# A two-layer trunk on one core: the memory's parts made in the FFN ahead of each mixer, another block order in first chunks, priorities on VectorE, narrower masks

## The chip, the cores and the metric

The kernel runs on one core of a Trainium2 chip, in one launch. The metric is the device time of that launch in microseconds (us); before the change it is 1129.36 us, the median of 3 runs (1125.65 to 1131.69). Engines are named as in the profile: PE is TensorE (matrix products), DVE is VectorE, ACT is ScalarE, POOL is GpSimd, and SP is SyncE, which issues the DMA transfers. DMA data go from HBM to SBUF; products land in PSUM, of which the kernel uses 8 banks.

## The reference

All values are float32: `x` is 1 x 256 x 1024, the memory `mem` 1 x 256 x 1024. Two layers run one after the other; layer 0 has a mixer of two attentions side by side, layer 1 multi-head latent attention. Cut to what matters here:

```
for layer in (0, 1):
    x = x + 0.5 * swiglu(rms_norm(x, ffn_norm[layer, 0]), ...)       # D_FF 2816
    h = rms_norm(x, mix_norm[layer])
    x = x + (diff_stickbreak_mixer(h, ...) if layer == 0 else mla_mixer(h, ...))
    x = x + memory_cross_attention(rms_norm(x, xm_norm[layer]), rms_norm(mem, xm_mem_norm[layer]), ...)
    x = x + 0.5 * swiglu(rms_norm(x, ffn_norm[layer, 1]), ...)

def rms_norm(x, gain):   return x * rsqrt(mean(x * x, -1) + 1e-6) * gain
def swiglu(h, wg, wu, wd):   return (silu(h @ wg) * (h @ wu)) @ wd
def memory_cross_attention(h, m, w_q, w_kv, ...):    # 4 heads of 128
    q = rms_norm(heads(h @ w_q));  k, v = split(m @ w_kv);  k = rms_norm(heads(k))
    return (softmax(q k^T / sqrt(128)) v) @ w_o
```

The mean of squares of the memory is the same in both layers; only the gain differs. In the chunk-causal softmax a query of chunk c (64 positions) sees the keys of chunks up to c, in query blocks of 128.

## The kernel before

**Exact products in three passes.** Every float32 factor is split into a high part in the chip's fp32r type and a low part, the rest. A block product is then three single-pass matmuls into one PSUM tile (`mm3`, L275 to L279): high x high (L276), high x low (L277) and low x high (L278). Weights come from HBM in pieces of 1 MB (`wr`); ACT casts the high part (`wh`, L240) and DVE subtracts (`wl`, L242; in the mixers POOL takes a quarter). There are two raw buffers (`RAW`), three pairs of high and low parts (`HL`), and a weight is asked for two ahead of its use (`LOOK`). The release of a weight's buffers by PE is thus what lets ACT begin with a later weight.

**Phases.** FFN, mixer, cross-attention, FFN in each layer. Read from the trace: the first FFN to 204 us, the first mixer to 339.6, its cross-attention to 381, the second FFN to 577, the FFN of layer 1 to about 765, the second mixer (MLA) to 893, its cross-attention to 934.6, the last FFN to the end. x is held as 8 blocks of 128 features x 256 positions. An FFN makes gate and up products in 11 pairs of chunks of 256 columns, then 8 down products; a chunk product is 2 column halves (j) x 8 row blocks (k) of `mm3`, in the order j = 0: k = 0 to 7, then j = 1 (`fm`, L584; in mixers the generator `fm_g`, L596).

**From one phase to the next.** The last products of a phase add to x block by block in `finish_dt` (L491): DVE adds the PSUM tile to x (L494), which also frees the PSUM bank; `split` makes the high part on ACT (`xh`, L471) and the low part on DVE (`xl`, L472) with the next norm's gain; ACT squares (L505) and POOL sums the squares over the blocks (L513). The norm's scale is applied behind the next product. `norm` (L522) sums the squares over partitions with PE (`colsum`, L465), DVE adds epsilon (L525), POOL takes the power (L457). `spread` (L531) brings the scale to all partitions: two diagonal matrices on DVE (L534), one product with ones on PE (L537), a copy by ACT (L539).

**Memory.** `mem_gain` (L755) loads the transposed memory in four transfers of 256 KB (L761) and splits its 8 blocks (L471, L472) into buffers named slotr. It is called in the mixers: in the first one behind the second product, in MLA at the first memory product. In the first mixer, ACT also squares the memory (L770), POOL adds the squares (L773, L776), and PE sums them over partitions in a task of its own (`colsum`, L465), of which the scale follows. The keys and values of the memory are then made in the mixers.

**Who sets the order.** In mixers and cross-attentions the PE order is written by a planner (`run`, L430): tasks are generators with a priority (lower first) and conditions; each event has an estimated time (tables `EST_*`), and of the tasks that may start by then, the one with the lowest priority goes next. On the other engines a scheduler orders the instructions, mostly as the code emits them; `tc.high_priority()` moves those inside it forward, and `keep_in_program_order` pins one to its place. Each engine works its queue strictly in that order, and so does SP with the transfers it issues.

**Masks.** `mask` (L308) writes -1e30 into the scores' tile by a product of two rows, ahead of the scores: for query block 0 (t = 0) 512 columns (L310), for block 1 256 columns (L312).

**Table.** ACT loads the table of the exponential and logarithm in the first mixer ahead of its use (L950). In MLA it is loaded at the first exponential (L729).

## Time and profile before

| | |
|---|---|
| median of 3 runs (lowest to highest) | 1129.36 us (1125.65 to 1131.69) |
| profiled execution, its own time | 1128.84 us |
| its span, from first to last instruction | 1127.1 us |
| granted PE clock, mean over the span | 0.997 of full |
| busy: PE, DVE, ACT, POOL | 1102.8, 776.8, 653.3, 199.8 us |
| share of the span: PE, DVE, ACT, POOL | 98%, 69%, 58%, 18% |
| moved by DMA | 192.44 MB, mean 171 GB/s |

How to read it: one execution was recorded instruction by instruction; the times in the rows below count from the span's start. A busy PE counts overlapping matmuls once. A wait is put down to the instruction that released it last. In timelines a row may join several instructions (xN) and gives start, duration, and in brackets the engine's idle time ahead and who ended it.

### The profile page before, as it was taken

The page shows a single profiled execution, that of the slowest core. Times are in us where ns is not written, and L with a number is a line of the kernel's source. Part 1 is how long each engine was busy: PE and PEld are TensorE (multiplying, and loading weights), DVE is VectorE, ACT ScalarE, POOL GpSimd, SP SyncE. Part 2 cuts the span into 40 slices and gives each one's busy share as a digit, 9 for nine tenths or more (in the row PEclk, how much of TensorE's full clock was granted, in tenths as well). Part 3 has the DMA queues.
Part 4 walks back from the last instruction along what each step waited for, and adds up shares of the span by engine and source line. Part 5 has one row for each costly group of instructions (what it writes and reads, how often), then busy time and mean ns, then how long its engine had stood idle before and what let it go on. Part 6 is the DMA issues. An engine that isn't in the chain of part 4 may idle for free.

```text
span 1127.1 us, 23381 instructions
## 1 busy us (share of the span) xinstructions
PE 1102.8 (98%) x9044; PEld 1083.6 (96%) x9044; DVE 776.8 (69%) x1865; ACT 653.3 (58%) x1771; POOL 199.8 (18%) x217
## 2 busy tenths in 40 slices
PE   8999999999999999999999999999989999999998
PEld 8999999898999999999999999999878999999998
DVE  6867665768876776675666766655788768676653
ACT  6655545676765665554555555546866566555542
POOL 2000001556343200000100000014861421000000
PEclk9999999999999999999999999999999999999999
DMA  8654545544454345555545454555341534555561
GB/s 299 220 195 176 188 170 184 192 140 151 121 166 163 129 171 187 187 179 183 195 172 207 169 198 167 191 178 192 108 145 45 164 135 148 190 187 188 178 210 62
DMA packets 50224, 192.44 MB, mean 171 GB/s; under 512 B 5696, under 2 KB 7360, under 8 KB 35008
## 3 DMA queue, kind: packets, MB, share of 16 engines
q1 hardware_dynamic: 50112, 190.94, 49.7%
q8 instruction: 71, 1.16, 0.4%
q14 instruction: 41, 0.34, 0.1%
HBM read 189.87 MB, written 1.05 MB: 169 GB/s over the span
## 4 chain that ended last, share of the span: by engine, by line
PE 83%; DVE 9%; ACT 2%; issue 2%; POOL 2%; DMA 1%; SPq 0%; DVEq 0%; POOLq 0%; ACTq 0%
PE mm L276 26%; PE mm L277 26%; PE mm L278 26%; DVE wl L242 4%; DVE xl L472 1%; DMA wr<-wflat 1%; PE t L742 1%; POOL sm L457 1%; ACT wh L240 1%; DVE x L494 1%; PE t L465 1%; PE s L880 0%; PE o L1452 0%; PE s L1419 0%; ACT xh L471 0%
## 5 line engine op out<-in xcount | busy, mean ns | idle before, releaser
L240 ACT CAST wh<-wr 128x256 fp32r<-128x256 f32 (+1 forms) x1216 | 440.0, 433 | 337.8 <-PE mm L277 307.9
L242 DVE TENSOR_TENSOR wl<-wr,wh 128x256 fp32r<-128x256 f32 (+1 forms) x1171 | 482.6, 470 | 117.9 <-ACT wh L240 112.8
L276 PE MATMUL mm<-xh,wh 128*128 128x256 f32 x1584 | 447.7, 283 | 4.3 <-DVE slotf L682 1.8
L277 PE MATMUL mm<-xl,wh 128*128 128x256 f32 x1584 | 445.5, 281 | 3.6 <-DVE xl L472 3.6
L278 PE MATMUL mm<-xh,wl 128*128 128x256 f32 x1584 | 445.6, 281 | 0.1
L276 PEld LDWEIGHTS mm<-xh,wh 128*128 128x128 f32 x1584 | 299.3, 189 | 5.5 <-issue 3.2
L277 PEld LDWEIGHTS mm<-xl,wh 128*128 128x128 f32 x1584 | 299.4, 189 | 4.6 <-DVE xl L472 4.4
L278 PEld LDWEIGHTS mm<-xh,wl 128*128 128x128 f32 x1584 | 299.2, 189 | 0.6 <-DVE wl L263 0.3
L276 PE MATMUL mm<-slotr,wh 128*128 128x256 f32 x896 | 252.4, 282 | 0.0
L277 PE MATMUL mm<-slotr,wh 128*128 128x256 f32 x896 | 251.4, 281 | 0.0
L278 PE MATMUL mm<-slotr,wl 128*128 128x256 f32 x896 | 251.4, 281 | 0.0
L276 PEld LDWEIGHTS mm<-slotr,wh 128*128 128x128 f32 x896 | 168.9, 188 | 0.4 <-issue 0.3
L277 PEld LDWEIGHTS mm<-slotr,wh 128*128 128x128 f32 x896 | 168.9, 189 | 0.1
L278 PEld LDWEIGHTS mm<-slotr,wl 128*128 128x128 f32 x896 | 168.9, 188 | 0.0
L513 POOL TENSOR_TENSOR acc<-acc,sq 128x256 f32<-128x256 f32 x49 | 40.5, 827 | 538.2 <-ACT sq L505 531.8
L242 POOL TENSOR_TENSOR wl<-wr,wh 128x512 fp32r<-128x512 f32 x45 | 67.7, 1505 | 108.8 <-ACT wh L240 108.7
L690 DVE TENSOR_TENSOR slotf<-mm,rb 128x512 f32<-128x512 f32 x44 | 30.4, 690 | 81.9 <-PE mm L278 81.9
L682 DVE TENSOR_TENSOR slotf<-mm,rb 128x512 f32<-128x512 f32 x44 | 30.4, 690 | 38.0 <-PE mm L278 38.0
L276 PE MATMUL mm<-wh,slotr 128*128 128x256 f32 (+2 forms) x176 | 55.5, 315 | 0.0
L471 ACT ACTIVATE xh<-x,gains 128x256 fp32r<-128x256 f32 x64 | 32.0, 506 | 39.2 <-DVE x L494 35.4
L278 PE MATMUL mm<-wh,slotr 128*128 128x256 f32 (+2 forms) x176 | 53.3, 303 | 0.0
L277 PE MATMUL mm<-wl,slotr 128*128 128x256 f32 (+2 forms) x176 | 53.1, 302 | 0.0
(192 smaller groups left out, 1095.7 us busy)
## 6 DMA issues: line engine op xcount, KB each, us to landing
wr<-wflat SPq DMA_DIRECT2D x118, 1024.0 KB, 4.8
wr<-wflat SPq DMA_DIRECT2D x180, 256.0 KB, 3.9
wr<-wflat SPq DMA_DIRECT2D x16, 768.0 KB, 4.3
slotf<-memT SPq DMA_DIRECT2D x8, 256.0 KB, 5.5
x<-xT SPq DMA_DIRECT2D x4, 256.0 KB, 4.6
wr<-wflat SPq DMA_DIRECT2D x2, 512.0 KB, 7.7
slotf<-xtok SPq DMA_DIRECT2D x4, 256.0 KB, 7.7
out<-x SPq DMA_DIRECT2D x8, 128.0 KB, 3.8
```

The source lines that it names most:

```text
L240: A.copy(hi[:, a:b], raw[:, a:b])
L242: e.tensor_tensor(out=lo[:, a:b], in0=raw[:, a:b], in1=hi[:, a:b].bitcast(F32), op=ALU.subtract)
L276: PE.matmul(out, a[0], b[0], start=first, stop=False, **kw)
L277: PE.matmul(out, a[0], b[1], start=False, stop=False, **kw)
L278: PE.matmul(out, a[1], b[0], start=False, stop=last, **kw)
L457: G.tensor_tensor(out=y, in0=v, in1=mhalf[:, 0:n], op=ALU.pow)
L465: PE.matmul(ps[:, 2 * c:2 * c + 2], b, ones[:, 0:2], start=k == 0, stop=k == len(blocks) - 1)
L471: return (A.activation(hi, src, AF.Identity, scale=g), V.scalar_tensor_tensor(out=lo, in0=src, scalar=g, in1=hi.bitcast(F32), op0=ALU.mult ...
L472: V.scalar_tensor_tensor(out=lo, in0=src, scalar=g, in1=hi.bitcast(F32), op0=ALU.mult, op1=ALU.subtract))
L513: G.tensor_tensor(out=st.acc, in0=st.acc, in1=sq, op=ALU.add)
L682: V.tensor_tensor(out=t.rearrange("p (a b) -> p a b", b=S), in0=pg.rearrange("p (a b) -> p a b", b=S), in1=rbb, op=ALU.mult)
L690: V.tensor_tensor(out=u.rearrange("p (a b) -> p a b", b=S), in0=pu.rearrange("p (a b) -> p a b", b=S), in1=rbb, op=ALU.mult)
```

## The change

Five things change.

1. **Memory.** The call of `mem_gain` moves into `ffn`: in the first FFN of each layer, after the pairs f = 2, 4, 6 and 8 (`MEM_AT`), a quarter of the memory is loaded and split, into eight tiles of its own that stay (`mem0h` to `mem3l`). For layer 0 a second copy of the memory, with positions on partitions (`memtok`), is loaded too (four transfers of 256 KB), and ACT squares it with the sum over the features taken along; two DVE instructions and a power on POOL give the scale. The adds on POOL, the column sums on PE and their task are gone. The arenas of the mixers have 11 slotr buffers instead of 19.
2. **Block order.** The first chunk of each phase (`gate` of f = 0 in an FFN but the very first, `qb` 0, `ckv`, `xq` 0) takes the blocks in the order EARLY: k = 0 to 4 of j = 0, k = 0 to 4 of j = 1, then k = 5 of both j, 6 of both, 7 of both.
3. **Priorities.** The update of x, its splits, the norm's DVE instructions and the scalings in `spread` are emitted with `tc.high_priority()`.
4. **Masks.** Only the columns that the mask changes are written: the last 64 of each 128 (t = 0) or of each 256 (t = 1): 256 and 128 columns.
5. **Table.** MLA asks for the exponential's table behind its first product; the scheduler puts it ahead of the last high part of x in the FFN before; the request in the first mixer stays.

The diff, cut to its core:

```diff
-SLOTS_MLA = (29, 19)
+SLOTS_MLA = (29, 11)          # SLOTS_MIX likewise
+MEM_AT = (2, 4, 6, 8)
...
     def mask(sp, t, b, n):
-        if t == 0:
-            PE.matmul(sp, mq[b:b + n], mk[b:b + n], start=True, stop=False, skip_group_check=True)
-        else:
-            PE.matmul(sp.rearrange("p (a b) -> p a b", b=S)[:, :, P:S], mq[b:b + n], mk[b:b + n, 0:S],
-                      start=True, stop=False, skip_group_check=True)
+        w = P if t == 0 else S
+        PE.matmul(sp.rearrange("p (a b) -> p a b", b=w)[:, :, w - 64:w], mq[b:b + n], mk[b:b + n, 0:512 * 64 // w],
+                  start=True, stop=False, skip_group_check=True)
...
     def finish_dt(dt, gc, ps=None, factor=1.0):
         xd = x[:, dt, :]
         if ps is not None:
-            V.scalar_tensor_tensor(out=xd, in0=ps, scalar=factor, in1=xd, op0=ALU.mult, op1=ALU.add)
+            with tc.high_priority():
+                V.scalar_tensor_tensor(out=xd, in0=ps, scalar=factor, in1=xd, op0=ALU.mult, op1=ALU.add)
...
-        made = split(h, l, xd, gcol(gc + dt))
         st.nxt[dt] = (h, l)
         if ps is None:
-            return made
+            return split(h, l, xd, gcol(gc + dt))
+        with tc.high_priority():
+            split(h, l, xd, gcol(gc + dt))
...          # norm (tensor_scalar, rsqrt) and spread (both scalings) likewise under high_priority
+    EARLY = [(j, k) for j in range(2) for k in range(KT - 3)] + [(j, k) for k in range(KT - 3, KT) for j in range(2)]
+    PLAIN = [(j, k) for j in range(2) for k in range(KT)]
-    def fm(w, xg, between=None):
+    def fm(w, xg, between=None, order=PLAIN):
         ps = ps_("mm")
-        for j in range(2):
-            if j and between:
+        for j, k in order:
+            if (j, k) == (1, 0) and between:
                 between()
-            for k in range(KT):
-                mm3(ps[:, j * S:(j + 1) * S], (w[0][:, j * KT + k, :], w[1][:, j * KT + k, :]),
-                    xg[k], k == 0, k == KT - 1)
+            mm3(ps[:, j * S:(j + 1) * S], (w[0][:, j * KT + k, :], w[1][:, j * KT + k, :]),
+                xg[k], j == k == 0 if order is EARLY else k == 0, k == KT - 1, skip_group_check=order is EARLY)
...          # fm_g likewise; callers pass EARLY for gate of f = 0, ("qb", 0), ("xq", 0), ckv
+    def mem_gain(l, q):
+        raw = al()
+        nc.sync.dma_start(raw.rearrange("p (a b) -> p a b", b=S), memT_d[:, 2 * q:2 * q + 2, :])
+        h, lo = mem_hl[2 * q:2 * q + 2]
...
+        for j in range(2):
+            sl_ = slice(j * S, (j + 1) * S)
+            split(h[:, sl_], lo[:, sl_], raw[:, sl_], gcol(G_MEM + l * KT + 2 * q + j))
+            memstate["x"].append((h[:, sl_], lo[:, sl_]))
+        rel(raw)
+        if l:
+            return
+        mt = al()
+        nc.sync.dma_start(mt, memtok_d[:, q // 2, (q % 2) * 512:(q % 2 + 1) * 512])
+        A.activation(mt, mt, AF.Square, accum_out=msum[:, q:q + 1])
...          # q == 3: tensor_reduce, tensor_scalar, rsqrt -> memstate["rs"]
     def ffn(l, j, gc, need_rb, mem=None):
...
+            if mem is not None and f in MEM_AT:
+                mem_gain(mem, MEM_AT.index(f))
...
-            ps = yield from fm_g("ckv", xg)
+            ps = yield from fm_g("ckv", xg, EARLY)
+            tc.keep_in_program_order(A.preload_act_table_set("natural_log_exp_and_others"))
```

Line numbers of the changed kernel are a few off: its `wl` is L243, its `mm3` L277 to L279, its update of x L495, the norm's DVE instruction L528, the scalings L538. Three places show what moves.

The first is VectorE at the start of the first mixer, around the spread. In the rows before, slotr from slotf are the memory's low parts, `sl_2669` is the norm's variance, L534 are the two scalings, and `wl` are weight splits:

```order
L472 SCALAR_TENSOR_TENSOR slotr_2705<-slotf_2679,gains,slotr_2704 128x256 x2
L525 TENSOR_SCALAR sl_2669<-t_2791 128x2
L472 SCALAR_TENSOR_TENSOR slotr_2707<-slotf_2682,gains,slotr_2706 128x256
L534 TENSOR_SCALAR slotf_2688<-cst,sl_2668 128x128
L242 TENSOR_TENSOR wl_2797<-wr_2796,wh_2798 128x512 x3
L534 TENSOR_SCALAR slotf_2688<-cst,sl_2668 128x128
L472 SCALAR_TENSOR_TENSOR slotr_2707<-slotf_2682,gains,slotr_2706 128x256
L472 SCALAR_TENSOR_TENSOR slotr_2709<-slotf_2684,gains,slotr_2708 128x256 x2
L472 SCALAR_TENSOR_TENSOR slotr_2711<-slotf_2686,gains,slotr_2710 128x256 x2
```

The same place in the changed kernel:

```order
L364 TENSOR_TENSOR nlam<-lam 128x1
L365 TENSOR_SCALAR nlam<-nlam 128x1
L528 TENSOR_SCALAR sl_2711<-t_2825 128x2
L538 TENSOR_SCALAR slotf_2721<-cst,sl_2710 128x128 x2
L243 TENSOR_TENSOR wl_2831<-wr_2830,wh_2832 128x512 x3
```

The memory's low parts are gone from here, and the two scalings stand together, ahead of the three weight splits that stood between them.

The second is TensorE in the first chunk of the second FFN, the gate product. Before, the block `xh_4997`, the last of x (k = 7), comes as the eighth `mm3`, and j = 1 starts behind it:

```order
L278 MATMUL mm_5063<-xh_4976,wl_4798 128x256
L276 MATMUL mm_5063<-xh_4997,wh_4799 128x256
L277 MATMUL mm_5063<-xl_4998,wh_4799 128x256
L278 MATMUL mm_5063<-xh_4997,wl_4798 128x256
L276 MATMUL mm_5063<-xh_4845,wh_4799 128x256
```

In the changed kernel, behind the fifth `mm3` (`xh_4930`, k = 4) the order goes back to the first block (`xh_4841`); the last block's `xh_4993` comes in the 15th and 16th `mm3`, at the chunk's end:

```order
L277 MATMUL mm_5059<-xh_4930,wh_4795 128x256
L278 MATMUL mm_5059<-xl_4931,wh_4795 128x256
L279 MATMUL mm_5059<-xh_4930,wl_4794 128x256
L277 MATMUL mm_5059<-xh_4841,wh_4795 128x256
L278 MATMUL mm_5059<-xl_4842,wh_4795 128x256
L279 MATMUL mm_5059<-xh_4841,wl_4794 128x256
```

The third is VectorE at the same phase's start: the updates of x (x from mm), the low parts of x (`xl`) and the splits of the next two weights. Before:

```order
L494 SCALAR_TENSOR_TENSOR x<-mm_4920,x 128x256
L242 TENSOR_TENSOR wl_4901<-wr_4900,wh_4902 128x256 x5
L472 SCALAR_TENSOR_TENSOR xl_4935<-x,gains,xh_4934 128x256
L494 SCALAR_TENSOR_TENSOR x<-mm_4941,x 128x256
L494 SCALAR_TENSOR_TENSOR x<-mm_4962,x 128x256
L472 SCALAR_TENSOR_TENSOR xl_4956<-x,gains,xh_4955 128x256
L494 SCALAR_TENSOR_TENSOR x<-mm_4983,x 128x256
L472 SCALAR_TENSOR_TENSOR xl_4977<-x,gains,xh_4976 128x256
L242 TENSOR_TENSOR wl_5044<-wr_5043,wh_5045 128x256
L472 SCALAR_TENSOR_TENSOR xl_4998<-x,gains,xh_4997 128x256
```

After:

```order
L495 SCALAR_TENSOR_TENSOR x<-mm_4916,x 128x256
L243 TENSOR_TENSOR wl_4897<-wr_4896,wh_4898 128x256 x3
L495 SCALAR_TENSOR_TENSOR x<-mm_4937,x 128x256
L472 SCALAR_TENSOR_TENSOR xl_4931<-x,gains,xh_4930 128x256
L243 TENSOR_TENSOR wl_4897<-wr_4896,wh_4898 128x256
L472 SCALAR_TENSOR_TENSOR xl_4952<-x,gains,xh_4951 128x256
L495 SCALAR_TENSOR_TENSOR x<-mm_4958,x 128x256
L243 TENSOR_TENSOR wl_4897<-wr_4896,wh_4898 128x256
L472 SCALAR_TENSOR_TENSOR xl_4973<-x,gains,xh_4972 128x256
L495 SCALAR_TENSOR_TENSOR x<-mm_4979,x 128x256
L243 TENSOR_TENSOR wl_5040<-wr_5039,wh_5041 128x256 x3
L472 SCALAR_TENSOR_TENSOR xl_4994<-x,gains,xh_4993 128x256
```

The update of the second of these four blocks (`x` from mm_4941 before, mm_4937 after) stands behind three weight splits of this stretch instead of five and behind no low part; the last low part stands behind three pieces of the weight after next instead of one.

## Rows read from the trace of the kernel before

**Rows 1.** The page, part 1: busy time, share of the span, instructions of each engine.

```profile
PE 1102.8 (98%) x9044; PEld 1083.6 (96%) x9044; DVE 776.8 (69%) x1865; ACT 653.3 (58%) x1771; POOL 199.8 (18%) x217
```

**Rows 2.** The waits of TensorE: who, for whom, us in total, times, longest.

```profile
PE mm L277 <- DVE xl L472: 3.6, 4, 1.0
PE s L1419 <- DVE slotf L1406: 2.7, 1, 2.7
...
PE t L742 <- DVE slotf L734: 2.0, 1, 2.0
...
PE mm L276 <- DVE x L494: 0.8, 2, 0.7
...
PE s L1034 <- ACT slotf L1059: 0.6, 1, 0.6
```

**Rows 3.** Timeline of TensorE, start of the first mixer: start, us, instruction, [idle before].

```profile
213.03 0.28 PE L278 MATMUL mm<-xh,wl 128*128 128x256 f32 x1
215.62 0.67 PE L537 MATMUL t<-slotf,ones 128*128 128x256 f32 x2 [2.31 <-issue]
```

**Rows 4.** Timeline of VectorE at the same place.

```profile
211.69 0.29 DVE L534 TENSOR_SCALAR slotf<-cst,sl 128x128 f32<-128x128 f32 x1 [0.61 <-POOL sl L457]
211.89 2.96 DVE L242 TENSOR_TENSOR wl<-wr,wh 128x512 fp32r<-128x512 f32 x3
214.78 0.74 DVE L534 TENSOR_SCALAR slotf<-cst,sl 128x128 f32<-128x128 f32 x1
```

**Rows 5.** Timeline of TensorE, the memory's column sums in the first mixer.

```profile
223.17 0.50 PE L465 MATMUL t<-ones,slotf 128*128 128x2 f32 x4
224.15 0.49 PE L1034 MATMUL s<-slotf,slotf 64*128 64x256 f32 x2 [0.48 <-DVE slotf L957]
```

**Rows 6.** Timeline of TensorE, start of the first cross-attention.

```profile
342.09 0.28 PE L276 MATMUL mm<-xh,wh 128*128 128x256 f32 x1
343.34 0.39 PE L277 MATMUL mm<-xl,wh 128*128 128x256 f32 x1 [0.97 <-DVE xl L472]
```

**Rows 7.** Stretches: busy us (instructions) of each engine, granted clock, DMA share, GB/s.

```profile
45.00:65.00 20.00, 20.00 (x171) 20.00 (x170) 13.81 (x35) 9.88 (x30) 0.00 (x0) 1.00 0.55 190
...
28.00:34.00 6.00, 5.09 (x30) 5.12 (x31) 6.00 (x16) 5.20 (x15) 0.30 (x2) 0.72 0.61 197
820.50:828.50 8.00, 5.35 (x26) 4.40 (x26) 6.13 (x11) 3.86 (x7) 6.87 (x7) 0.79 0.59 189
```

**Rows 8.** Groups by line, 204 to 222 us: busy us, mean ns | idle before.

```profile
L472 DVE SCALAR_TENSOR_TENSOR slotr<-slotf,gains,slotr 128x256 fp32r<-128x256 f32 x8 | 5.5, 742 | 3.1 <-ACT slotr L471 3.1
L776 POOL TENSOR_TENSOR slotf<-slotf,slotf 128x256 f32<-128x256 f32 x6 | 5.4, 895 | 0.4
...
L471 ACT ACTIVATE slotr<-slotf,gains 128x256 fp32r<-128x256 f32 x8 | 3.7, 498 | 2.7 <-DMA slotf<-memT 2.7
```

**Rows 9.** Timeline of TensorE, masks of 512 and of 256 columns in MLA.

```profile
824.78 0.38 PE L312 MATMUL s<-mk,mq 128*128 128x256 f32 x1
824.98 0.61 PE L1419 MATMUL s<-slotf,slotf 96*128 96x256 f32 x1
...
834.19 0.48 PE L310 MATMUL s<-mk,mq 128*128 128x512 f32 x1
834.51 0.50 PE L1419 MATMUL s<-slotf,slotf 96*128 96x128 f32 x3
```

**Rows 10.** Timeline of ScalarE, the first exponentials of MLA.

```profile
827.95 1.28 ACT L729 ACT_TABLE_LOAD   x1 [2.85 <-DVE sm L723]
```

**Rows 11.** Groups by line, 45 to 105 us in the first FFN.

```profile
L240 ACT CAST wh<-wr 128x256 fp32r<-128x256 f32 x84 | 27.9, 402 | 27.6 <-PE mm L277 25.9 <-issue 1.6
```

**Rows 12.** Groups by line, 0 to 60 us: squares of x at the start.

```profile
L1494 ACT ACTIVATE slotf<-slotf 128x512 f32<-128x512 f32 x4 | 2.5, 619 | 0.0
```

**Rows 13.** Groups by line, 762 to 776 us: the memory's low parts in MLA.

```profile
L472 DVE SCALAR_TENSOR_TENSOR slotr<-slotf,gains,slotr 128x256 fp32r<-128x256 f32 x8 | 3.4, 476 | 3.1 <-ACT slotr L471 3.1
```

**Rows 14.** The page, part 6: transfers, KB each, us from issue to landing.

```profile
slotf<-memT SPq DMA_DIRECT2D x8, 256.0 KB, 5.5
```

More of the change, by code (lines that the diff above doesn't have):

```diff
@@ L68 @@
 HL = 3
[L69 removed]
+SLOTS_MIX = (29, 11)
+MEM_AT = (2, 4, 6, 8)
 def _cols(w, c0, c1):
@@ L326, in rows @@
             return rows_a[:, c0:c0 + w] if c0 < 384 else rows_b[:, c0 - 384:c0 - 384 + w]
-        for dst, c0, w in ((mq, C_MQ, P), (mk, C_MK, 512), (ntri, C_TRI, P)):
+        for dst, c0, w in ((mq, C_MQ, P), (mk, C_MK, S), (ntri, C_TRI, P)):
             tmp = al()
@@ L524, in norm @@
             v = st.var
-            V.tensor_scalar(out=v, in0=cs, scalar1=1.0 / D, scalar2=EPS, op0=ALU.mult, op1=ALU.add)
-            rsqrt(v, 2, st.rs)
+            with tc.high_priority():
+                V.tensor_scalar(out=v, in0=cs, scalar1=1.0 / D, scalar2=EPS, op0=ALU.mult, op1=ALU.add)
+                rsqrt(v, 2, st.rs)
             return ps
@@ L532, in spread @@
         dg = al()
-        for t in range(2):
-            V.tensor_scalar(out=dg[:, t * P:(t + 1) * P], in0=ident, scalar1=st.rs[:, t:t + 1],
-                            scalar2=None, op0=ALU.mult)
+        with tc.high_priority():
+            for t in range(2):
+                V.tensor_scalar(out=dg[:, t * P:(t + 1) * P], in0=ident, scalar1=st.rs[:, t:t + 1],
+                                scalar2=None, op0=ALU.mult)
         ps = get("t")
@@ L598, in fm_g @@
         ps = take("mm")
-        for j in range(2):
-            for k in range(KT):
-                mm3(ps[:, j * S:(j + 1) * S], (w[0][:, j * KT + k, :], w[1][:, j * KT + k, :]),
-                    xg[k], k == 0, k == KT - 1)
-                if k % 4 == 3 and (j, k) != (1, KT - 1):
-                    yield {}
+        for i, (j, k) in enumerate(order):
+            mm3(ps[:, j * S:(j + 1) * S], (w[0][:, j * KT + k, :], w[1][:, j * KT + k, :]),
+                xg[k], j == k == 0 if order is EARLY else k == 0, k == KT - 1, skip_group_check=order is EARLY)
+            if i % 4 == 3 and i < 2 * KT - 1:
+                yield {}
         done(key)
@@ L669, in ffn @@
         for f in range(FT // 2):
-            pg = fm_first(xg) if ("gate", l, j, f) == FIRST else ahead or fm(weight(("gate", l, j, f), P), xg)
+            pg = (fm_first(xg) if ("gate", l, j, f) == FIRST else
+                  ahead or fm(weight(("gate", l, j, f), P), xg, order=PLAIN if f else EARLY))
             ahead = None
@@ new lines, in trunk_kernel @@
+    mem_hl = [cpool.tile([P, 512], F32R, name=f"mem{q}{h}") for q in range(4) for h in "hl"]
+    memstate["rs"] = cpool.tile([P, 2], F32, name="rmem")
+    msum = cpool.tile([P, 4], F32, name="msum")
+    def mem_gain(l, q):
+        raw = al()
+        nc.sync.dma_start(raw.rearrange("p (a b) -> p a b", b=S), memT_d[:, 2 * q:2 * q + 2, :])
+        h, lo = mem_hl[2 * q:2 * q + 2]
+        if q == 0:
+            memstate["x"] = []
+        for j in range(2):
[8 more added lines that the diff above has]
+        A.activation(mt, mt, AF.Square, accum_out=msum[:, q:q + 1])
+        rel(mt)
+        if q == 3:
+            v = sm()[:, 0:2]
+            V.tensor_reduce(out=v, in_=msum.rearrange("p (a b) -> p a b", b=2), axis=AX.X, op=ALU.add)
+            V.tensor_scalar(out=v, in0=v, scalar1=1.0 / D, scalar2=EPS, op0=ALU.mult, op1=ALU.add)
+            rsqrt(v, 2, memstate["rs"])
@@ L854, in products @@
             for c in range(2):
-                ps = yield from fm_g((f"xq{l}", c), xg)
+                ps = yield from fm_g((f"xq{l}", c), xg, PLAIN if c else EARLY)
                 q = al()
@@ L947, in products @@
                 for c in range(2):
-                    ps = yield from fm_g((key, c), xg)
+                    ps = yield from fm_g((key, c), xg, EARLY if (key, c) == ("qb", 0) else PLAIN)
                     if (key, c) == ("qb", 0):
@@ L971, in products @@
                     c = int(key[1])
-                    yield from (mem_k(0, c, [ev["rm"]]) if key[0] == "k" else
-                                mem_v(0, c, memstate["v"], Event(), [ev["rm"]]))
+                    yield from (mem_k(0, c, []) if key[0] == "k" else
+                                mem_v(0, c, memstate["v"], Event(), []))
                     continue
@@ L1359, in mem_product @@
         def mem_product(c):
-            if c == 0:
-                mem_gain(1, ev)
             yield from mem_k(1, c, [])
-            if c == 1 and not MEM_KEEP:
-                rel(*memstate.pop("tiles"))
         def mem_values(c):
@@ L1527, in _constants @@
             c[:, cs + t * d:cs + (t + 1) * d] = np.concatenate([-sin[r], sin[r]], 1)
-    kk = np.arange(512)
     for row in (0, 64):
         c[row, C_MQ:C_MQ + 64] = -1e30
-        c[row, C_MK:C_MK + 512] = kk % 128 >= 64
+        c[row, C_MK:C_MK + S] = 1.0
     return c
```

70 lines of the change are left out of this document (11 added, 59 removed).

## The prediction

> **What bounds the kernel now.** I read the page's busy times first: TensorE is busy for 98% of the span [rows 1], so time is gained only where TensorE waits, or from what it executes. The second view is the list of TensorE's waits [rows 2]. The reader is to see that no wait there is longer than 2.7 us, and that most are for results of VectorE. Third come timelines of places where the change acts: the start of the first mixer [rows 3, 4], the memory's column sums there [rows 5], and the start of a cross-attention [rows 6]. Inside an FFN TensorE never waits: from 45 to 65 us it is busy for all 20.00 us with 171 matmuls [rows 7], so one 128x256 matmul comes every 20.00/171 = 0.117 us. A wait costs the distance between the two starts around it, less this pace.
>
> The sum is made against the profiled execution, 1128.84 us (the span of 1127.1 and 1.74 around it), which is 0.5 below the median of 1129.36.
>
> **Start of the first mixer.** The spread matmul of L537 starts 215.62 − 213.03 = 2.59 us after its predecessor [rows 3], 2.47 more than the pace. It needs both diagonal scalings of L534. The first runs at 211.69, the second at 214.78, behind 2.96 us of weight splits [rows 4]; ahead of them VectorE and GpSimd work off the memory's splits and squares [rows 8]. The change puts both scalings right behind the norm. Started together at 211.69 at the latest, they end by 211.69 + 2 × 0.29 = 212.3, before TensorE comes to the spread at 213.03 + 0.12. Term: −2.47. What is late next is the weight split behind them, by 0.29 us, for a weight whose product is still to come.
>
> The column sums of the memory's squares (L465) and the wait behind them leave TensorE: 224.15 − 223.17 = 0.98 us [rows 5]. The scores behind them waited 0.48 us for VectorE; four more blocks of three matmuls (12 × 0.117 = 1.4 us) now stand ahead of them and cover that. Term: −0.98.
>
> The planner puts the rest of this mixer in another order. The largest other wait there that the list names is 0.6 us (L1034 for L1059 [rows 2]), the best case if it goes. The worst that I can bound is one new wait as long as the longest on a VectorE result, 2.7 us [rows 2]. I take −0.4, near the best: VectorE and GpSimd have eight splits and seven additions less there, and no row shows the new wait.
>
> **Starts of four phases.** In the two cross-attentions and the two second FFNs, one matmul of the first chunk waits for the low part of the last block of x: 3.6 us over 4 waits [rows 2]. Between starts one of them costs 343.34 − 342.09 − 0.12 = 1.13 for a named wait of 0.97 [rows 6], so 0.16 comes on top of each: 3.6 + 4 × 0.16 = 4.24. Before, block 7 is due after 7 blocks of three matmuls; in the order of after it is due after 14, so 7 × 3 × 0.117 = 2.46 us later. The longest of the four waits is 1.0 [rows 2], and where the chunk itself starts earlier it is by 0.8 at most (next term): 0.6 us are in hand, even if no split comes earlier. The order of after also puts VectorE's updates and splits of x ahead of weight splits. Blocks 5 and 6 are due after 10 and 12 blocks instead of 5 and 6, 1.8 and 2.1 us later, and before neither was waited for. Term: −4.24.
>
> The first matmul of both second FFNs waits for an update of x that frees its PSUM bank: 0.8 named over 2 waits, the longest 0.7 [rows 2], with 0.16 each on top 1.12. The order of after puts that update behind six weight splits instead of eight and a split of x, over 1 us earlier. Term: −1.12. Late next are the weight splits that these pass, a few pieces, for a product that starts 48 × 0.117 = 5.6 us after the chunk.
>
> **Masks.** Of the 18 mask matmuls, 6 shrink from 512 columns to 256 and 12 from 256 to 128. A 512-column one is followed 0.32 us later, a 256-column one 0.20 us later [rows 9]: 0.12 less. One of the six stands ahead of the 2.7 us wait, which swallows it: 5 × 0.12 = 0.60. For 128 columns there is no row: each gives 0.06 (half of 0.12) if columns set the pace and 0 if what follows does, so the 12 give 0 to 0.72. I take half; together −0.96, bounds −0.6 to −1.32.
>
> **Table load in the second mixer.** ACT loads its table for 1.28 us once its wait for VectorE is over, and the first exponential stands behind it [rows 10]. The order of after has the load in the FFN before, ahead of the last split of x. TensorE's wait of 2.0 us for the normalised result (L734) [rows 2] hangs on these exponentials, but L734 also stands behind weight splits on VectorE. Bounds 0 and −1.28; I take −0.8, since the order of after also moves L734 ahead of a weight split. In the FFN the load delays ACT by 1.28 us, where in 60 us it idles 27.6 for TensorE [rows 11].
>
> **Work added to the FFNs.** For two layers × 8 blocks of the memory: 16 high parts on ACT at 0.50 us [rows 8] and 16 low parts on VectorE; four squares of 0.62 us [rows 12] with their sums read on ACT; 8 + 4 transfers of 256 KB. The low part took 0.74 us in the first mixer, beside GpSimd's additions [rows 8], and 0.48 us in the second, without them [rows 13]. In the FFN GpSimd does nothing [rows 7], so I take 0.48. The Trainium skill (SBUF — State Buffer, section Who interferes with whom) says that a VectorE instruction with two SBUF inputs contends with a GpSimd instruction that reads SBUF. Both rows agree, and by it the price in the FFN is 0.48; by the first mixer's row it would be 16 × 0.26 = 4.2 us more of VectorE's time, as hidden as the rest. One call costs ACT 1.0 to 1.8 us and VectorE 1.0 us. From 45 to 65 us ACT is busy for 9.88 of 20 us and VectorE for 13.81 [rows 7], and ACT's idle time ends with TensorE's release of a weight buffer, at least one product (5.6 us) ahead of that weight's use. Term: 0. From the second mixer the same splits vanish: also 0, since no wait of TensorE stands there, and the later 2.7 us wait (L1419 for L1406) hangs on a chain whose order is not changed.
>
> **Sum.** −2.47 − 0.98 − 0.4 − 4.24 − 1.12 − 0.96 − 0.8 = −10.97; 1128.84 − 10.97 = 1117.9, forecast 1118.
>
> **Rivals.**
> A, the waits come back in part. Only half of the 5.36 us at the four starts goes, because the wait moves to another block or to a weight split that was passed, and the first mixer's new order costs 2.7 where I have −0.4. Then 1117.9 + 2.68 + 3.1 = 1123.7; with one of the two, 1120.6 or 1121.0. For it: the planner's times for that order are estimates, and a low part there can take twice as long beside GpSimd. Against: the time in hand above.
> B, the other side: in-order blocking in the FFN. A memory transfer lands 5.5 us after its issue [rows 14], and ACT's high part waits for it with the weight's casts behind it, for which VectorE and then TensorE wait. ACT idles 27.6 us before 84 casts [rows 11], which are 10.5 weights, 2.6 us each. If nothing else hid it, each of the 8 calls would stop TensorE for 5.5 − 2.6 = 2.9 us: 1117.9 + 23.2 = 1141. It decides for slower from (11.0 + 5.6)/8 = 2.1 us per call. Against: the 5.6 us between a weight's casts and its use, and a share of 0.55 of the DMA engines at 190 GB/s [rows 7]; 3.1 MB more at 190/0.55 = 345 GB/s are 9.1 us of their time over two FFNs. The Trainium skill (Trainium Kernel Development and Optimization, section Key Constraints) says that transfers of all queues run on the same 16 engines and interleave, so by it a memory transfer also lengthens a weight's landing; no row of before shows the two together inside an FFN, and that is why B is not nearer 0.
> C, the clock: TensorE's granted clock averages 0.72 in 28 to 34 us and 0.79 in 820.5 to 828.5 [rows 7], which is about 3.4 us at the lower level (1.2 GHz) in each, after waits of TensorE. Where work fills them they cost half, 1.7 us. If they go, 1116.2 (one) or 1114.5 (both). Against: the waits ahead of both are not touched.
>
> **How the numbers follow.** Forecast 64% (its own range 1115.5 to 1120, from the bounds of masks, table and planner), A 17%, B 6%, C 13%. Low end: C's 1114.5 less the unused bounds 0.2 + 0.36 + 0.48, rounded down to 1113. High end: A's 1123.7 and a table load that gives nothing, +0.8: 1124.5. A measurement of this kernel tells some 0.5%, 5.6 us, from no change. Faster than 1123.7 are the forecast, C and nearly all of A, of which and of the forecast I leave some to unforeseen losses: 0.85. Within: A's end and a mild B, 0.10. Slower: B, 0.05.
>
> **What would show it.** Right: the spread matmul and the four starts follow their predecessors at 0.12 to 0.2 us; no column sum among the first mixer's products; no table load between the second mixer's first scores and exponentials; TensorE at 20.00 of 20 us through FFNs with memory splits. A gap at block 5 of a first chunk or at new places of the first mixer shows A; gaps at a gate or up product behind a memory split show B; PEclk of 1.00 around 30 or 825 us shows C. The forecast is wrong if equal FFN stretches grow, or if the mixers' gaps keep their sum.

## The result, and the profile after

| | before | after |
|---|---|---|
| median of 10 runs (lowest to highest) | 1129.15 us (1125.12 to 1133.07) | 1133.88 us (1132.32 to 1138.06) |
| profiled execution: span | 1127.1 us | 1131.2 us |
| busy: PE, DVE, ACT, POOL | 1102.8, 776.8, 653.3, 199.8 us | 1111.9, 767.8, 655.0, 192.5 us |

The ratio of the times is 1.0053, 95% interval 1.0035 to 1.0071: the change made the kernel 0.5% slower, where a gain of 11 us had been forecast. The time lies outside the range of 1113 to 1124.5.

The waits that were to go are gone. This is the list of TensorE's waits in the changed kernel (who, for whom, us in total, times, longest):

```profile
PE s L1405 <- DVE slotf L1392: 2.6, 1, 2.6
PE t L752 <- DVE slotf L812: 2.2, 2, 2.0
PE s L312 <- ACT slotf L739: 2.0, 3, 0.8
...
PE o L1064 <- issue: 0.7, 1, 0.7
PE o L1064 <- ACT slotf L976: 0.5, 1, 0.5
PE t L752 <- DVE slotf L744: 0.5, 1, 0.5
```

No wait for xl, for an update of x or for the spread is left of [rows 2, 3], and the wait for the normalised result (L734 before, L744 now) fell from 2.0 to 0.5. New are 2.2 us for L812 (a memory key's scaling), 2.0 for L739 (exponentials) and 1.2 of two kinds ahead of L1064. The spread's matmul, [rows 3] before, now follows its predecessor after 0.12 us, in the timeline of TensorE:

```profile
211.96 0.29 PE L279 MATMUL mm<-xh,wl 128*128 128x256 f32 x1
212.08 0.59 PE L541 MATMUL t<-slotf,ones 128*128 128x256 f32 x2
```

What nobody had asked about is the pace where TensorE never waits. Stretches (busy us with instruction counts in the order PE, PEld, DVE, ACT, POOL, then granted clock, DMA share, GB/s), first of the change, then of before at the second and third stretch (the first is in [rows 7]):

```profile
45.00:65.00 20.00, 20.00 (x169) 20.00 (x169) 16.55 (x42) 12.79 (x39) 0.00 (x0) 1.00 0.68 232
28.00:34.00 6.00, 6.00 (x52) 6.00 (x51) 4.88 (x13) 4.35 (x13) 1.97 (x8) 1.00 0.77 263
...
400.00:420.00 20.00, 20.00 (x169) 20.00 (x169) 14.21 (x37) 11.43 (x34) 0.00 (x0) 1.00 0.55 205
960.00:980.00 20.00, 20.00 (x169) 20.00 (x168) 14.27 (x35) 10.99 (x32) 0.00 (x0) 1.00 0.52 180
```

```profile
400.00:420.00 20.00, 20.00 (x171) 20.00 (x170) 14.39 (x36) 11.51 (x35) 0.00 (x0) 1.00 0.57 211
960.00:980.00 20.00, 20.00 (x172) 20.00 (x172) 15.22 (x38) 12.04 (x36) 0.00 (x0) 1.00 0.56 199
```

TensorE is busy for 20.00 of 20 us at a granted clock of 1.00 in both, and yet 169 matmuls fit where 171 or 172 did. The counts take in the matmuls that overlap an end of the stretch; from one recorded start to the next a matmul took 120.0 ns in the change's FFNs, 118.7 ns in the first three FFNs of before and 117.4 in its last. One or two per cent more on each matmul stand in no list of waits, but the kernel has about 9,000 matmuls.

The phases in the two traces, each from the last update of x ahead of it to its own last one, the first from the first matmul on (us), and the part that the pace alone makes (matmuls at the regular pace in the change, times the difference of the mean distances):

| phase | before | after | difference | of it pace | rest |
|---|---|---|---|---|---|
| start and first FFN | 200.52 | 199.26 | -1.26 | +2.06 | -3.3 |
| first mixer | 138.98 | 141.08 | +2.10 | -0.09 | +2.2 |
| cross-attentions, both | 83.93 | 82.76 | -1.17 | +0.58 | -1.7 |
| second FFN of each layer | 376.90 | 378.27 | +1.37 | +6.24 | -4.9 |
| first FFN of layer 1 | 188.66 | 191.00 | +2.34 | +2.11 | +0.2 |
| second mixer | 133.66 | 134.66 | +1.00 | +0.26 | +0.7 |
| sum | 1122.65 | 1127.02 | +4.4 | +11.2 | -6.8 |

So there are two questions: what made the pace (11.2 us), and why the rest is -6.8 and not -11.0.

### The profile page after: what moved, and what is told of

The parts are those of the page before. It is cut to its first block, busy times and chain, and to the rows that moved or that the text cites. A ratio compares the mean times of both kernels' runs of the same rounds, so it can differ in the third digit from the quotient of the medians.

```text
span 1131.2 us, 23382 instructions
## 1 busy us (share of the span) xinstructions
PE 1111.9 (98%) x9040; PEld 1093.7 (97%) x9040; DVE 767.8 (68%) x1866; ACT 655.0 (58%) x1775; POOL 192.5 (17%) x210
## 4 chain that ended last, share of the span: by engine, by line
PE 89%; DVE 4%; ACT 3%; POOL 2%; issue 1%; DMA 1%; SPq 0%; DVEq 0%; ACTq 0%; POOLq 0%
PE mm L279 28%; PE mm L277 28%; PE mm L278 28%; ACT slotf L739 1%; PE t L752 1%; POOL sm L457 1%; DVE wl L243 1%; PE s L1405 1%; DMA wr<-wflat 1%; PE t L465 1%; PE s L877 0%; PE o L1438 0%; POOL sl L457 0%; PE o L896 0%; DVE sm L730 0%
## 5 line engine op out<-in xcount | busy, mean ns | idle before, releaser
L243 DVE TENSOR_TENSOR wl<-wr,wh 128x256 fp32r<-128x256 f32 (+1 forms) x1171 | 480.3, 465 | 136.2 <-ACT wh L241 131.1
L277 PE MATMUL mm<-xh,wh 128*128 128x256 f32 x1584 | 449.5, 284 | 1.6 <-ACT wh L241 1.4
L279 PE MATMUL mm<-xh,wl 128*128 128x256 f32 x1584 | 448.3, 283 | 0.1
L277 PEld LDWEIGHTS mm<-xh,wh 128*128 128x128 f32 x1584 | 297.8, 188 | 2.5 <-ACT wh L241 1.6
L279 PEld LDWEIGHTS mm<-xh,wl 128*128 128x128 f32 x1584 | 296.5, 187 | 0.4 <-DVE wl L264 0.3
L277 PE MATMUL mm<-slotr,wh 128*128 128x256 f32 x896 | 254.0, 283 | 0.3 <-ACT slotr L471 0.3
L279 PE MATMUL mm<-slotr,wl 128*128 128x256 f32 x896 | 253.4, 283 | 0.0
L277 PEld LDWEIGHTS mm<-slotr,wh 128*128 128x128 f32 x896 | 168.3, 188 | 1.0 <-ACT slotr L471 0.6
L279 PEld LDWEIGHTS mm<-slotr,wl 128*128 128x128 f32 x896 | 167.8, 187 | 0.0
L243 POOL TENSOR_TENSOR wl<-wr,wh 128x512 fp32r<-128x512 f32 x45 | 66.8, 1485 | 114.3 <-ACT wh L241 105.6
L739 ACT ACTIVATE slotf<-s,sm,sl 128x256 f32<-128x256 f32 (+1 forms) x64 | 32.8, 522 | 23.6 <-DVE sm L733 18.0
L495 DVE SCALAR_TENSOR_TENSOR x<-mm,x 128x256 f32<-128x256 f32 x64 | 26.7, 418 | 28.4 <-PE mm L279 28.4
L472 DVE SCALAR_TENSOR_TENSOR xl<-x,gains,xh 128x256 fp32r<-128x256 f32 x64 | 35.8, 564 | 5.2 <-ACT xh L471 5.2
```

The costliest lines, as they stand in the source:

```text
L243: e.tensor_tensor(out=lo[:, a:b], in0=raw[:, a:b], in1=hi[:, a:b].bitcast(F32), op=ALU.subtract)
L277: PE.matmul(out, a[0], b[0], start=first, stop=False, **kw)
L279: PE.matmul(out, a[1], b[0], start=False, stop=last, **kw)
L472: V.scalar_tensor_tensor(out=lo, in0=src, scalar=g, in1=hi.bitcast(F32), op0=ALU.mult, op1=ALU.subtract))
L495: V.scalar_tensor_tensor(out=xd, in0=ps, scalar=factor, in1=xd, op0=ALU.mult, op1=ALU.add)
L739: A.activation(p[:, i * w:(i + 1) * w], sps[:, i * w:(i + 1) * w], AF.Exp, bias=nb[:, i:i + 1], scale=r, accum_out=sums[:, i:i + 1])
```

## The experiments

Each run was compared with the kernel before on the same chip; that kernel's medians in these comparisons were 1125.8, 1125.5, 1128.0 and 1125.7 us.

**Where the pace comes from.** The first suspect was the place in SBUF. The eight new memory tiles (16 KB) stand ahead of x's parts, and a narrower mask constant, a smaller tile for the memory's scale and a new one for its sums shift everything behind them by an amount that is no multiple of 128: `xh`, `xl` and all slots begin 96 bytes behind a multiple of 128 in the change, 32 in before. The weights' high and low parts begin at a multiple of 128 in both. These places are worked out from the sizes of the tiles in the kernels; no trace holds addresses. I call the difference, modulo 128, the distance: 96 and 32. Three kernels change it and nothing else (in the traces their instructions stand in the same order on all engines); a fourth undoes the block order and keeps the distance.

```diff
-    msum = cpool.tile([P, 4], F32, name="msum")
+    msum = cpool.tile([P, 20], F32, name="msum")[:, 0:4]     # a_pad64; [P, 12] in a_pad32
```

> The changed kernel with 64 more bytes of SBUF ahead of x's parts and of the slots; no instruction is moved. In the trace of the change, equal stretches of an FFN without any wait hold 169 matmuls in 20 us where 171 stood before (120.0 ns against 118.7 a matmul): some 10 us over the kernel. Theory P (place): this comes from where xh, xl and the slots lie against the weights, 96 bytes behind a multiple of 128 now and 32 before. It expects 118.7 ns or less again here and 1123 to 1125 us. Rival Q (order): it comes from the instruction stream, the new order or the added work. It expects 169 matmuls in 20 us and 1133 to 1135 us as for the change.

Measured: 1120.72 us, ratio to before 0.9961 (0.9940 to 0.9983), where the change has 1.0053. The medians are 13 us apart, but they come from two comparisons in which before itself differs by 3.3 us (1129.15 and 1125.82); by the ratios the 64 bytes are worth some 10 us.

> As the one before with 32 bytes more instead of 64: the parts of x and the slots begin at multiples of 128 bytes, where neither kernel had them. Theory P expects a pace of its own, not that of the change; if full alignment is the best, under 118.7 ns and under 1123 us. Rival Q expects 120.0 ns and 1133 to 1135 us.

Measured: 1123.48 us, ratio 0.9983 (0.9964 to 1.0002), 118.7 ns a matmul: not the pace of the change, but that of before. Full alignment is not the best.

```diff
-            memstate["rs"] = cpool.tile([P, 32], F32, name="rmem")[:, 0:2]
+            memstate["rs"] = cpool.tile([P, 16], F32, name="rmem")[:, 0:2]     # in the kernel before
```

> The kernel before with 64 bytes less ahead of x's parts and of the slots (96 behind a multiple of 128, as in the change); no instruction is moved. Theory P expects 120.0 ns a matmul (169 in 20 us) in the FFNs and about 1129 + 10 = 1139 us. Rival Q expects no difference from before: 171 in 20 us, 1129 us.

Measured: 1138.06 us, ratio 1.0111 (1.0081 to 1.0141). 64 bytes less in an unused part of a tile cost the kernel before 12 us. One stretch of each, the change with 64 bytes more first, then before with 64 less:

```profile
400.00:420.00 20.00, 20.00 (x171) 20.00 (x170) 14.15 (x35) 10.85 (x32) 0.00 (x0) 1.00 0.54 180
```

```profile
400.00:420.00 20.00, 20.00 (x169) 20.00 (x168) 13.94 (x34) 11.11 (x33) 0.00 (x0) 1.00 0.54 178
```

171 and 169 matmuls in 20 us: the pace went with the place, in both directions and to the count that was expected.

```diff
-                  ahead or fm(weight(("gate", l, j, f), P), xg, order=PLAIN if f else EARLY))
+                  ahead or fm(weight(("gate", l, j, f), P), xg, order=PLAIN))     # and the three calls of fm_g
```

> The changed kernel with every first chunk in the block order of before; everything else, the places in SBUF too, as in the change. Theory P expects 120.0 ns a matmul still, and at the four phase starts a wait for the last low part again, shorter than the 1.1 us of before by what the priorities give: 0.3 to 1.1 us each, so 1135 to 1138 us. Rival Q, if the block order made the pace, expects 118.7 ns and about 1125 us.

Measured: 1141.90 us, ratio 1.0143 (1.0114 to 1.0172), 120.0 ns a matmul; the waits at the four starts are back, at the upper end of what was expected:

```profile
PE mm L278 <- DVE xl L472: 4.3, 4, 1.1
...
PE mm L277 <- ACT xh L471: 1.1, 2, 0.6
```

The time is above the expected range. Against the change's profile the four phases with these starts take 7.2 us more, the first mixer, whose first chunk went back too, 1.5, and the start with the first FFN 0.7. In this mixer the granted clock is 0.83 from 306 to 316 us, where the change's is 1.00 throughout, so its 1.5 us are not put down to the order.

Theory Q (instruction order or added work) has fallen: the order went back and the pace stayed, the order stayed and the pace went back.

**The place of x's parts, or their distance from the weights?** Three more kernels, the first as a_pad64 with [P, 28], the other two with a dummy tile ahead of everything:

```diff
+    zpool = ctx.enter_context(tc.tile_pool(name="z", bufs=1))
+    zpool.tile([P, 16], F32, name="z")          # a_front64; [P, 8] in a_front32
     wpool = ctx.enter_context(tc.tile_pool(name="w", bufs=1))
```

> The changed kernel with 96 bytes more ahead of x's parts and the slots: they begin 64 bytes behind a multiple of 128 (96 in the change, 32 in before, 0 with 32 bytes more). Theory P1 (only the place 96 is bad) expects 118.7 ns a matmul (171 in 20 us) and 1121 to 1124 us. Theory P2 (the half of a 128-byte line decides: 64 and 96 slow, 0 and 32 quick) expects 120.0 ns (169 in 20 us) and about 1133 us.

Measured: 1113.14 us (1108.35 to 1117.43), ratio 0.9875 (0.9838 to 0.9913), 117.8 ns a matmul. Both theories were wrong: 64 is the quickest distance tried.

> The changed kernel with 64 bytes ahead of everything: weights at 64 behind a multiple of 128, x's parts and slots at 32, so their distance is that of the change, while x's parts lie as in before. If the place of x's parts by itself sets the pace: 118.7 ns a matmul and 1121 to 1125 us. If the distance between x's parts and the weights sets it: 120.0 ns and about 1133 us.

Measured: 1133.06 us, ratio 1.0065 (1.0041 to 1.0088), 120.0 ns.

> The changed kernel with 32 bytes ahead of everything: weights at 32 behind a multiple of 128, x's parts and slots at 0; the distance is again that of the change. Place of x's parts by itself: 118.7 ns, 1121 to 1125 us. Distance: 120.0 ns, about 1133 us. If the place of the weights has a price of its own, a pace that neither run has shown.

Measured: 1133.38 us, ratio 1.0070 (1.0042 to 1.0097), 120.0 ns. Weights and x's parts moved together keep the pace of the change, though x's parts then lie where the quicker kernels had them, and the ratios stay near the change's 1.0053. So neither place by itself sets the pace; what these kernels share is the distance. Moving both was tried at this one distance.

A last kernel of this kind gives the two operands of one FFN different distances: 64 bytes ahead of the slots alone, so that the gate and up products (x's parts) keep 96 and the down products (slots) have 32.

```diff
         with tc.tile_pool(name=nm("ar"), bufs=1) as pool:
+            pool.tile([P, 16], F32, name=nm("gap"))
```

> The changed kernel with 64 bytes in front of the slots alone: xh and xl stay at 96 behind a multiple of 128 (as in the change), the slots, which hold the factors of the down products, lie at 32 (as in before); weights at 0. Theory P (each product's own distance sets its pace) expects within one FFN 120.0 ns a matmul in the gate and up products (first 125 us of an FFN) and 118.7 ns in the down products. Rival P3 (the engine falls into one rhythm for the whole kernel, by its first products or by another tile's place) expects one pace in both.

Measured: 1130.17 us, ratio 1.0019 (0.9988 to 1.0050). Two stretches of its first FFN, gate and up products at 60 us and down products at 140:

```profile
60.00:80.00 20.00, 20.00 (x169) 20.00 (x169) 16.33 (x41) 13.73 (x42) 0.00 (x0) 1.00 0.67 228
140.00:160.00 20.00, 20.00 (x172) 20.00 (x172) 12.62 (x34) 10.06 (x31) 0.74 (x1) 1.00 0.52 176
```

169 and 172: within one FFN the pace changes with the operand (120.0 ns, then 117.3 here and 118.7 in the other three FFNs). So each product's own distance acts, at once; the rival of one rhythm for the whole kernel has fallen.

**The first mixer.** Without the column sums' task the planner put TensorE's products there in another order. This kernel (distance 32) gives the planner back a task that takes the same time and bank in its plan, and executes nothing; TensorE's order is then that of before, less the column sums.

```diff
+        def gate():
+            yield dict(t=1, lat=6.0)
+            ps = take("t")
+            spend(0.44)
+            drop(ps, 0.6)
+            signal(ev["rm"], 1.6)
...
+                    if (key, c) == ("qb", 1):
+                        spawn(0, gate())
...          # mem_k and mem_v of this mixer wait for ev["rm"] in the plan, as in before
```

> The changed kernel with 64 bytes more as in the first of these runs (1120.7 us), and a task without work in the first mixer's plan that takes the time of the column sums there, so that TensorE's order is that of before without the column sums. Theory O (the planner's other order made the first mixer's new waits, 7.7 us where before had 1.4): the first mixer takes 6 us less than the 140.9 of the run with 64 bytes, and the kernel about 1115 us. Rival (the waits come from what ScalarE and VectorE do there, such as higher priorities): the waits stay, 1120 to 1121 us.

Measured: 1114.63 us, ratio 0.9889 (0.9867 to 0.9910). The mixer takes 135.75 us against 140.87. TensorE's waits inside it, of the change (204 to 340 us) and of this kernel (198 to 334):

```profile
PE t L752 <- DVE slotf L812: 2.0, 1, 2.0
PE s L312 <- ACT slotf L739: 1.6, 2, 0.8
PE o L1064 <- issue: 0.7, 1, 0.7
PE o L1064 <- ACT slotf L976: 0.5, 1, 0.5
```

```profile
PE s L1036 <- ACT slotf L1061: 0.6, 1, 0.6
```

4.8 us of waits against 0.6 (L1036 is the wait of L1034 in [rows 2]); the change has two more of 0.4 and 0.3 there. The rival is out: priorities and memory splits are the same in both. Some of the 6 us between the two kernels' medians may be rhythm: in this profile the two middle FFNs ran at 117.3 ns, and with 64 bytes more all four at 118.7.

**The priorities.** The kernel with 64 bytes more, without the four `tc.high_priority()`.

```diff
-            with tc.high_priority():
+            if True:          # all four places
```

> The changed kernel with 64 bytes more (1120.7 us), without the four high priorities; the block order stays. Theory E (the block order alone takes the waits at the phase starts, having 0.6 us in hand without any earlier split) expects the four starts without a wait and 1120 to 1122 us, at most 1 to 2 us from the first mixer's spread if its scalings fall behind weight splits again. Rival (the priorities are what takes the waits) expects waits of 0.5 to 1.1 us at the four starts and 1123 to 1126 us.

Measured: 1122.93 us, ratio 0.9954 (0.9926 to 0.9982). No wait for xl at the four starts, as theory E expected, and 0.3 us for updates of x. What came back is a wait at the start of the kernel:

```profile
PE mm L277 <- DVE slotf L690: 2.6, 1, 2.6
...
PE mm L277 <- DVE x L495: 0.3, 2, 0.2
```

Start and first FFN take 200.16 us against 197.03 with the priorities: in this pair their worth is there, not where they were expected to help. In the ten profiles with the priorities and the new masks this wait is 0.3 us at most.

The first mixer's spread does not need the priorities either. Without them the second scaling (L538) stands behind three weight splits again, as in [rows 4], and yet ends before TensorE comes to the spread (L541):

```profile
208.43 2.99 DVE L243 TENSOR_TENSOR wl<-wr,wh 128x512 fp32r<-128x512 f32 x3
211.34 0.27 DVE L538 TENSOR_SCALAR slotf<-cst,sl 128x128 f32<-128x128 f32 x1
```

```profile
212.69 0.28 PE L279 MATMUL mm<-xh,wl 128*128 128x256 f32 x1
212.80 0.59 PE L541 MATMUL t<-slotf,ones 128*128 128x256 f32 x2
```

So another of the edits takes this wait. The likely one is the move of the memory, whose splits and squares stood ahead of the scalings before [rows 8]; it was not tried apart from the rest.

The two medians (1122.93 and 1120.72) are from different comparisons and are not told apart by their runs; the wait at the start is.

**All together.** The distance 64 and the first mixer's order of before.

> The quickest distance (64 bytes, 1113.1 us) and TensorE's order of before in the first mixer (1114.6 us with the distance 32) together. If the two gains add: the first mixer 5 us less than the 140.3 of the run with 96 bytes more, and about 1108 us, quicker than both kernels. Rival (the order's gain hangs on the pace and is lost beside it): 1113 us.

Measured: 1110.49 us (1103.79 to 1112.03), ratio 0.9825 (0.9785 to 0.9864): quicker than both kernels. The mixer takes 134.85 us against 140.31, as the first theory expected; the median lies between the two theories' 1108 and 1113.

Last, masks and table load of before in that kernel: the old `mask` and `mk`, and no `preload_act_table_set` in the second mixer.

> The quickest kernel so far (1110.5 us; second mixer 133.5 us from the last update of x before it to its own) with the masks and the table load of before: 512 and 256 columns, and the table loaded at the first exponential of the second mixer. If the terms of the prediction stand (masks -0.96, of which some 0.6 in this mixer, and load -0.8): the second mixer takes 134.9 us and TensorE's wait of 2.0 us for the normalised result is back. Rival (what both give is taken back by the next wait there): the second mixer stays at 133.5 within 0.3 us, and the kernel at 1110 us.

Measured: 1109.03 us, ratio 0.9850 (0.9804 to 0.9897), second mixer 133.23 us against 133.54. The time does not tell the two kernels apart: the intervals of their ratios (0.9850 and 0.9825) overlap, and the first FFN of this profile ran at a pace of its own (below). In the second mixer, one profile each, the rival was right: nothing is lost there without both edits. The wait for the normalised result is back (L746 here, L744 with both edits), and what it costs is made up elsewhere. TensorE's waits and the granted clock in this mixer, first with the old masks and load (743.6 to 876.9 us), then with the new (746 to 879.5):

```profile
PE t L754 <- DVE slotf L746: 2.0, 1, 2.0
...
PE o L1448 <- DVE slotf L762: 0.6, 2, 0.4
```

```profile
743.60:876.90 133.30, 124.37 (x936) 114.96 (x935) 95.38 (x223) 88.01 (x206) 66.99 (x74) 1.00 0.38 119
```

```profile
PE o L1447 <- DVE slotf L760: 0.9, 2, 0.5
...
PE t L752 <- DVE slotf L744: 0.5, 1, 0.5
...
PE s L312 <- ACT slotf L739: 0.4, 1, 0.4
```

```profile
746.00:879.50 133.50, 125.41 (x934) 115.96 (x933) 95.18 (x223) 87.08 (x205) 68.52 (x74) 0.99 0.38 119
```

2.6 us of these waits against 1.8, so the edits save 0.8 of waits; but with them TensorE is busy 1.0 us longer (125.41 against 124.37) for narrower masks, and the granted clock is 0.99 of full in this mixer against 1.00. The change and before differ in the same way from 820 to 840 us, 0.83 after and 0.91 before:

```profile
820.00:840.00 20.00, 17.20 (x99) 16.01 (x99) 14.47 (x41) 11.84 (x29) 12.93 (x17) 0.83 0.49 158
```

```profile
820.00:840.00 20.00, 15.55 (x88) 13.83 (x87) 17.88 (x44) 15.03 (x37) 14.43 (x17) 0.91 0.48 158
```

That the clock takes the gain back is not shown. A profile is one execution, and the executions of one kernel differ in clock: over before's 22 runs in one comparison the mean granted clock goes from 0.994 to 1.000. Nor is this mixer longer where its clock is lower, in three kernels whose instructions stand in the same order and run at the same pace. These are the second mixer in the change, then with everything moved by 32 bytes, then by 64:

```profile
763.40:898.05 134.65, 127.94 (x932) 118.16 (x932) 94.29 (x223) 87.13 (x206) 67.24 (x74) 0.97 0.36 118
```

```profile
763.70:898.22 134.52, 127.86 (x932) 118.08 (x932) 94.21 (x222) 87.22 (x206) 67.53 (x74) 0.97 0.37 118
```

```profile
766.12:901.67 135.55, 126.19 (x932) 117.06 (x932) 95.14 (x223) 87.07 (x206) 67.63 (x74) 0.99 0.37 117
```

The highest clock goes with the longest mixer, and 1 us lies between kernels of one order. A difference of 0.3 us between two profiles is within that; why the saved waits don't show in the mixer's time stays open.

The first FFN of the kernel with the old masks shows something else, a stretch of it, then the same of the kernel with the new:

```profile
100.00:120.00 20.00, 20.00 (x179) 20.00 (x178) 15.97 (x40) 11.94 (x35) 0.00 (x0) 1.00 0.52 182
```

```profile
100.00:120.00 20.00, 20.00 (x172) 20.00 (x172) 15.06 (x38) 11.14 (x33) 0.00 (x0) 1.00 0.52 180
```

179 and 172 matmuls at the same distance: 113.3 and 117.8 ns.

## Why the prediction was wrong

The step that failed first is the one that looked safest: "Inside an FFN TensorE never waits: from 45 to 65 us it is busy for all 20.00 us with 171 matmuls [rows 7], so one 128x256 matmul comes every 20.00/171 = 0.117 us", carried over to the changed kernel as a constant. It is not one. New tiles moved x's parts and the slots from distance 32 to 96 to the weights, and the pace went from 118.7 (in the last FFN 117.4) to 120.0 ns. That is 11.2 us between the two profiles (2 of them because before's last FFN ran at 117.4 and not at 118.7), no term of the sum had it, and no rival did. Only the prediction's last sentence did, as a sign without a cause: "The forecast is wrong if equal FFN stretches grow". "TensorE at 20.00 of 20 us through FFNs with memory splits" held, and showed nothing.

Point by point, from the column "rest" of the table:

- **First mixer**, forecast -2.47 (spread) - 0.98 (column sums) - 0.4 (order) and about 0.36 of the masks, -4.2; measured +2.2. The first two terms were right in size: neither wait is there [rows 3, 5]. For the spread the reason given, "The change puts both scalings right behind the norm", was not the one that counted: without the priorities the second scaling stands behind weight splits again and the wait stays away. The term "I take -0.4, near the best" was wrong in sign: the order cost some 5 us (140.87 against 135.75, and at distance 64 140.31 against 134.85), beyond its upper bound of 2.7, because it made several waits and I had bounded one. Rival A named this, with too small a price.
- **Four phase starts**, forecast -4.24 - 1.12 = -5.36; the rest is -1.7 - 4.9 = -6.6. Right, and by the mechanism named: undoing the block order alone brings back 4.3 + 1.1 us of waits, and leaving out the priorities brings back 0.3. "The order of after also puts VectorE's updates and splits of x ahead" added little.
- **Masks and table load**, forecast -0.96 and -0.8; in the second mixer, +0.7 measured and nothing gained in the experiment. Each local step happened: of the 2.0 us for L734 0.5 is left, and a 128-column mask is followed after 0.14 us where 256 columns took 0.20 (in the change it starts at 842.72 us and the scores behind it at 842.86). Part of the gain is gone again in a wait of a mask for L739 (0.4); where the rest went stays open. The masks' term was also a little large: in the first mixer masks start in pairs (two of 512 columns at 279.63 us, the scores 0.33 later), so a pair saves once, and the same working gives -0.8 in place of -0.96.
- **Work added to the FFNs**, forecast 0: the FFN of layer 1, which got the memory splits and nothing else, differs by +0.2 beside the pace. Rival B has fallen, though its first step happened: from 45 to 105 us ScalarE stood idle 3.7 us for the memory and 3.5 for its second copy, and its idle time ahead of the weights' casts is 13.8 us where it was 27.6 [rows 11], 7.5 of it now for the weights' own transfers. This stayed within ScalarE's idle time: no wait of TensorE in the FFNs stands behind a memory split. The transfers of the memory landed in 3.2 us (median) where 5.5 had been feared.
- **Start of the kernel**, forecast 0; the rest is -3.3. A wait of TensorE of 1.8 us for the first scaled gate product (L682) is gone, and the granted clock in 28 to 34 us is 1.00, 0.72 before [rows 7]. The wait is back without the priorities (2.6), and with them where the masks are the old ones (2.9): both move VectorE's work there, and which instruction decides was not tried. Rival C looked half right: in these profiles this stretch at the lower level went and the other, around 825 us, grew. But before with 64 bytes less and the change without the priorities wait 2.4 and 2.6 us at the start with a granted clock of 1.00 from 28 to 34 us, so that the clock went up because the wait went is not shown.

At the distance of before the change is worth 1125.82 - 1120.72 = 5.1 us, and 10.9 (1125.53 - 1114.63) with the mixer's order kept. The second is the forecast's size, largely by luck: the start's gain stands where those of masks and table were put, and two FFNs of its profile ran at 117.3 ns in place of 118.7, which is some 4 us (an estimate: 2 x 1,584 matmuls x 1.4 ns).

The forecast's "own range 1115.5 to 1120, from the bounds of masks, table and planner" does not come out of these bounds: they give 1117.9 - 0.2 - 0.36 - 0.48 = 1116.9 and, with the planner's 2.7, 1117.9 + 0.36 + 0.8 + 3.1 = 1122.2. The stated range of 1113 to 1124.5 does not hang on it.

## What to carry to other kernels

A kernel that is bound by TensorE without waits is still priced by its pace, so read the distance between starts in a stretch without waits before and after, not the busy share. A change that adds, drops or resizes a tile moves every tile behind it; compare the places of the matmul operands in both kernels, and try some padding before judging the change. And where a planner writes the order, a task that is taken out of the plan is a change of order everywhere behind it: keep its place in the plan and try both.

## What the runs showed of the hardware

| distance, bytes modulo 128 | ns a matmul in FFNs | kernels |
|---|---|---|
| 96 | 120.0 | the change 1133.88, before less 64 bytes 1138.06, 1133.06 and 1133.38 with all moved |
| 32 | 118.7 or 117.3 | before, 1120.72, 1122.93, 1114.63 |
| 0 | 118.7 | 1123.48 |
| 64 | 117.8 or 113.3 | 1113.14, 1110.49, 1109.03 |

The times are medians of different comparisons, in which before itself took 1125.5 to 1129.2 us. For 128x256 products of fp32r, with a weight load ahead of each, the time of one went with the distance between the two operands' places in SBUF: 2% from 117.8 to 120.0 ns, and 6% to the quickest rhythm, 113.3, which was seen in one FFN of one profile. At 32 and 64 there are two rhythms. One execution keeps one through a whole FFN and can change in a mixer, as before's profile does ahead of its last FFN; the runs of two of these kernels spread over 8 to 9 us (1116.83 to 1125.40, 1108.35 to 1117.43), at distance 0 over 2.7 us. Rhythm may be a part of that spread; the clock is another (0.994 to 1.000 in before's 22 runs). What picks the rhythm, and why 64 bytes matter, stays open: no run tells. Of the distances only four were tried, 32 bytes apart, always with high and low parts of the weights at the same place modulo 128. By the sizes of the tiles they lie within one stretch of 128 bytes, whole KB aside; so that the pace repeats every 128 bytes is my way of counting and not shown.
